# The last eighth of a down projection and the final norm, by halves of the tokens

## The chip, the cores and the metric

The kernel runs on one core of one Trainium2 chip. The metric is the device time of one execution in microseconds. The profile is one execution recorded instruction by instruction; its span reaches from the first to the last instruction.

## The reference

One layer of a hybrid block over 512 tokens of width 2048: a mixer of two recurrent head groups, a cross attention, and a squared-ReLU MLP, each added to the residual `h`, and a final norm. Only its end matters here:

```python
hn = _rmsnorm(h, norm_mlp[l])
h = h + jnp.square(jax.nn.relu(hn @ mlp_w_up[l])) @ mlp_w_down[l]     # 2048 -> 8192 -> 2048
return _rmsnorm(h, norm_final)        # h * rsqrt(mean(h*h) + eps) * gain, over the 2048 channels
```

## The kernel before

Activations lie transposed: channels on the 128 partitions, the 512 tokens along the free dimension. The residual is 16 tiles `hres[n]` (128 channels x 512 tokens, float32, `h` in the profile). All large products run in a reduced float32 format, made accurate by splitting: an operand becomes a high part `hi` (a cast, `split`, line 132, on ScalarE) and a low remainder `lo` (a subtraction, line 133, on VectorE), and a product is the sum of three matmuls: weights high by tokens high, weights high by tokens low, weights low by tokens high. All matmuls go through `mm` (line 124), so one line of the profile holds them all, and the output's name tells the stage.

`wload` (from line 150) brings one weight tile of 128 x 1024 float32 (512 KB) on the SyncE queue into one of three `wraw` buffers and splits it into `whi` and `wlo`, two buffers each. `gemm` runs the 24 matmuls of a group: 8 blocks of 128 input channels, three matmuls of 512 columns each, all into one accumulator `dn` in PSUM.

The MLP's up stage (`strassen`, output `up`) works by quarters of 256 tokens or channels and writes squared activations to DRAM (`Ud`). The down stage (`dn`) has eight eighths `e` of the 8192 hidden channels. Each eighth has 16 groups `n`, one for each residual tile; a group ends with a VectorE add of the accumulator to `hres[n]` (line 1485). While an eighth runs, `usplit` (line 1454) reads the eight token tiles of the next one from DRAM and splits them into `uh` and `ul` (128 x 512 each).

The final norm follows the last eighth: `finish` (lines 1241 to 1247) squares `hres[n]` on ScalarE and adds it to `acc` on VectorE; it starts for a tile as soon as that tile is complete. A matmul with a matrix of ones sums `acc` over the partitions (`pss`). `rsq` (lines 127 and 128) makes the reciprocal root by Ln and Exp on ScalarE, which loads a function table before each of them. Then 16 scalings on VectorE (line 1497) write to buffers `sl`, of which there are three, and SyncE stores each (line 1499, 256 KB).

The order of instructions on each engine is fixed when the kernel is built: the framework orders them by a schedule of its own, so that an operation without late inputs can come well ahead of its place in the source. An engine runs its list in order. The queue of SyncE holds loads and stores in one order; a DMA issued by ScalarE stands in ScalarE's list.

Line 1304 is the softmax exponential of the cross attention (`pr`), which uses the column tile `rcol`; line 1312 are the transposes `ptr` behind it, line 1314 their copies `phi`, and `at` is the product that uses these. The names `kp` and `sc` stand for matmuls of earlier stages.

Of the kernel before, what the change touches and what calls it, by code (L numbers as in the profile page):

```python
# [11 lines left out]
AF = mybir.ActivationFunctionType  # L12
ALU = mybir.AluOpType
# [4 lines left out]
P = 128  # L18
T = 512
M = 256  # L20
KD = 16
# [52 lines left out]
def build(tc, I, out):  # L74
    nc = tc.nc
    V, S, GP, PE = nc.vector, nc.scalar, nc.gpsimd, nc.tensor
# [19 lines left out]
    def K(name):  # L96
        o, w = CST[name]
        return cst0[:, o:o + w] if o < NC0 else cst[:, o - NC0:o - NC0 + w]

    def col(name, i=0):  # L100
        o, w = PRM[name]
        return prm[:, o + i:o + i + 1]
# [5 lines left out]
    ident, ones = K("ident"), K("ones")  # L108

    def cbias(v, nm):  # L110
        t = pc.tile([P, 1], F32, name=f"cb_{nm}")
        V.memset(t, float(v))
        return t

    b_eps6 = cbias(1e-6, "e6")
    b_gn = cbias(64e-5, "gn")
    b_one = cbias(1.0, "one")
    b_lq = cbias(-0.5 * math.log(128.0), "lq")

    def psb(nm, tag="mx", bufs=2):  # L120
        return tile_of(ps, [P, 512], F32, tag, nm, bufs)

    def mm(o, l, r, start=True, stop=True):
        PE.matmul(o, l, r, start=start, stop=stop)  # L124

    def rsq(o, x, scale, eps):
        S.activation(o, x, AF.Ln, bias=eps, scale=scale)
        S.activation(o, o, AF.Exp, scale=-0.5)

    def split(src, hi, lo, gain=None):  # L130
        if gain is None:
            S.copy(hi, src)  # L132
            V.tensor_tensor(out=lo, in0=src, in1=hi.bitcast(F32), op=ALU.subtract)  # L133
        else:
            S.activation(hi, src, AF.Copy, scale=gain)
            V.scalar_tensor_tensor(out=lo, in0=src, scalar=gain, in1=hi.bitcast(F32),
                                   op0=ALU.mult, op1=ALU.subtract)
# [4 lines left out]
    def wraw():  # L142
        wcnt[0] += 1
        return tile_of(pw, [P, 1024], F32, "wraw", f"wraw{wcnt[0]}", NWR)

    def wsplit():
        return (tile_of(pw, [P, 1024], F32R, "whi", f"whi{wcnt[0]}", NWS),
                tile_of(pw, [P, 1024], F32R, "wlo", f"wlo{wcnt[0]}", NWS))

    def wload(src):  # L150
        raw = wraw()
        nc.sync.dma_start(raw if len(src.shape) == 2 else raw.rearrange("p (a b) -> p a b", b=P), src)
        hi, lo = wsplit()
        split(raw, hi, lo)
        return hi, lo

    def gemm(pt, wsrc, nk, hi, lo):
        for h in range(nk // 8):
            wh, wl = wload(wsrc[:, h * 1024:(h + 1) * 1024] if nk > 8 else wsrc)
            for kk in range(8):  # L160
                k = h * 8 + kk
                sl = slice(kk * P, (kk + 1) * P)
                mm(pt, wh[:, sl], hi[k], start=(k == 0), stop=False)
                mm(pt, wh[:, sl], lo[k], start=False, stop=False)
                mm(pt, wl[:, sl], hi[k], start=False, stop=(k == nk - 1))
# [10 lines left out]
    def tile_of(pool, shape, dt, tag, nm, bufs):  # L176
        t = pool.tile(shape, dt, tag=tag, name=nm, bufs=bufs)
        turns[tag] = turns.get(tag, -1) + 1
        slot[t.tensor.name] = (tag, turns[tag] % bufs)
        holder[tag, turns[tag] % bufs] = t.tensor.name  # L180
        return t
# [156 lines left out]
    def act_tile(nm, dt=F32R):  # L338
        return tile_of(pa, [P, 512], dt, "act", nm, 32)
# [5 lines left out]
    rstd = pc.tile([P, T], F32, name="rstd")  # L345
# [6 lines left out]
    def tl(tag, w=512, bufs=1, shape=None):  # L352
        cnt[0] += 1
        return tile_of(pm, shape or [P, w], F32, tag, f"{tag}_{cnt[0]}", bufs)
# [53 lines left out]
    acc = tl("r")  # L408
# [763 lines left out]
    hres = [ph.tile([P, T], F32, tag=f"h{k}", name=f"h{k}", bufs=1) for k in range(16)]  # L1172
# [4 lines left out]
    def sl2(w=512):  # L1177
        cnt[0] += 1
        return ph.tile([P, 512], F32, tag="sl", name=f"sl{cnt[0]}", bufs=3)[:, 0:w]
# [18 lines left out]
    for n2 in range(8):  # L1198
        hi, lo = act_tile(f"vhi{n2}"), act_tile(f"vlo{n2}")
        for i in range(2):  # L1200
            n = 2 * n2 + i
            pt = psb(f"vp{n}", "mm", 2)
            for h in range(2):
                wh, wl = wload(I["wv"][n][:, h * 1024:(h + 1) * 1024])
                for k in range(h * 8, h * 8 + 8):
                    sl = slice(k % 8 * P, k % 8 * P + P)
# [6 lines left out]
            u, t = rstd[:, M:2 * M], sl2(M)  # L1213
# [7 lines left out]
    for g in range(4):  # L1221
        for h in range(4):
            pts = [psb(f"vo{g}_{h}_{mt}", ("mm", "mg")[h % 2]) for mt in range(2)]
            for q in range(2):
                wh, wl = wload(I["wo"][g, h][:, q * 1024:(q + 1) * 1024])
                for mt in range(2):
                    for e in range(2):
                        d = q * 2 + e
                        sl = slice(e * 512, e * 512 + 512)
# [11 lines left out]
    def finish(n, acc):  # L1241
        if n == 0:
            S.activation(acc, hres[n], AF.Square)
        else:
            sq = sl2()
            S.activation(sq, hres[n], AF.Square)
            V.tensor_tensor(out=acc, in0=acc, in1=sq, op=ALU.add)

    acc = ph.tile([P, T], F32, tag="acc", name="acc1", bufs=1)
    hh_, hl_ = [], []  # L1250
    for n in range(KD):
        xr = sl2()
        nc.sync.dma_start(xr, I["xT"][:, n, :])
        pt = psb(f"op{n}", "mm", 2)
        gemm(pt, I["w_out"][n], KD, oh, ol)
        V.tensor_tensor(out=hres[n], in0=pt, in1=xr, op=ALU.add)
        hi, lo = act_tile(f"hh{n}"), act_tile(f"hl{n}")
# [7 lines left out]
    rcol = pc.tile([P, 4], F32, name="rcol")  # L1265
# [9 lines left out]
    for g in range(2):  # L1275
        pts = [psb(f"sc{g}_{t}", ("mm", "mm", "mg", "mg")[t]) for t in range(4)]
        for n2 in range(8):
# [4 lines left out]
            wh = pw.tile([P, 1024], F32R, tag="whi", name=f"kqh{cnt[0]}", bufs=NWS)  # L1282
            wl = pw.tile([P, 1024], F32R, tag="wlo", name=f"kql{cnt[0]}", bufs=NWS)
            split(raw, wh, wl)
            for i in range(2):
                n = 2 * n2 + i
# [21 lines left out]
        for e in range(2):  # L1308
            for mt in range(2):
                pt = psb(f"ptr{g}_{e}_{mt}")  # L1310
# [9 lines left out]
    HA, HB = slice(0, M), slice(M, 2 * M)  # L1320
# [100 lines left out]
    acc = ph.tile([P, T], F32, tag="acc", name="acc2", bufs=1)  # L1421
    alloc(range(7))
    for n in range(KD):
        pt = psb(f"at{n}", "mm", 2)
# [18 lines left out]
    pu_cm = tc.tile_pool(name="pu", bufs=1, reuse_waits="tile")  # L1443
    pu = pu_cm.__enter__()
    uhl = [], []

    def usplit(f):
        if f >= 8:
            r = sl2()
        elif f % 2:  # L1450
            r = ph.tile([P, T], F32, tag="acc", name=f"ur{f}", bufs=1)
        else:
            r = pu.tile([P, T], F32, tag="ur", name=f"ur{f}", bufs=1)
        nc.sync.dma_start(r, Ud[f // 2][:, f % 2, :])
        hi, lo = act_tile(f"uh{f}"), act_tile(f"ul{f}")
        split(r, hi, lo)
        uhl[0].append(hi)
        uhl[1].append(lo)

    for p in range(32):  # L1460
        def square(i, half, c):
            t = c[:, half]
            V.scalar_tensor_tensor(out=t, in0=t, scalar=0.0, in1=rstd[:, half], op0=ALU.max, op1=ALU.mult)
            S.activation(t, t, AF.Square)
            if half is HA:
                nc.scalar.dma_start(Ud[p][:, i, :], c)

        def used(i):
            if p == 0 and i == T2:
                pt = psb("pss2")  # L1470
                mm(pt, ones, acc)
                rsq(rstd, pt, 1.0 / 2048, b_eps6)
            if p == 31 and i in (T1, T2, T3):
                for f in (range(0, 3), range(3, 6), range(6, 8))[i - T1]:
                    usplit(f)

        strassen(f"up{p}", (pu, 1024), [I["w_up"][p, i] for i in range(4)], list(range(8)), square, used)
    for e in range(8):
        uh, ul = uhl[0][e * 8:], uhl[1][e * 8:]
        for n in range(KD):  # L1480
            if e < 7 and n % 2 == 0:
                usplit(e * 8 + 8 + n // 2)
            pt = psb(f"dn{e}_{n}", "mm", 2)
            gemm(pt, I["w_dn"][e, n], 8, uh, ul)
            V.tensor_tensor(out=hres[n], in0=hres[n], in1=pt, op=ALU.add)  # L1485
    pu_cm.__exit__(None, None, None)


    acc = ph.tile([P, T], F32, tag="acc", name="acc3", bufs=1)
    for n in range(KD):  # L1490
        finish(n, acc)
    pt = psb("pss3")
    mm(pt, ones, acc)
    rsq(rstd, pt, 1.0 / 2048, b_eps6)
    for n in range(KD):
        o = sl2()
        V.scalar_tensor_tensor(out=o, in0=hres[n], scalar=col("norm_final", n), in1=rstd,
                               op0=ALU.mult, op1=ALU.mult)
        nc.sync.dma_start(out[n], o)
    es.close()  # L1500


# [96 lines left out]
```

## Time and profile before

| | us |
|---|---|
| median of 3 runs | 3080.55 (3079.55 to 3081.78) |
| the profiled execution, its own time | 3079.48 |
| its span | 3077.7 |
| mean granted TensorE clock | 0.994 |
| down stage, last matmul's end | 3053.2 |

How to read it: a row of the groups has line, engine, operation, output from inputs, shape and count, then total busy time and the mean of one in ns. A row of the chain or the timeline has the start and the length in us. A row of the windows has busy time (and count) for TensorE, its weight loads, VectorE, ScalarE and GpSimd, then the granted clock, the busy share of the DMA engines and GB/s. Matmuls overlap in the pipeline, so what a matmul costs in a stream is the distance of starts, not its length.

### The profile page before, as it was taken

What the parts mean: (1) busy time and instruction counts of PE and PEld (TensorE: products, weight loads), DVE (VectorE), ACT (ScalarE), POOL (GpSimd) and SP (SyncE); (2) the same over time, 40 slices, a digit from 0 to 9 for tenths busy, and PEclk for the clock granted to TensorE, in tenths of its full rate; (3) what the DMA queues carried; (4) which work ended last, traced back from release to release, by engine and by line L of the source; (5) the groups of instructions that cost most, each with busy time, mean ns of one, the idle gap of its engine ahead of it and who ended that gap; (6) DMA issues with size and microseconds to landing.
All of it is one profiled execution on the core that took longest, in us unless ns stands there. A gap on an engine that the chain in (4) does not pass through costs nothing.

```text
span 3077.7 us, 50561 instructions
## 1 busy us (share of the span) xinstructions
PE 3021.3 (98%) x20598; PEld 2603.3 (85%) x20598; DVE 1923.3 (62%) x2619; ACT 1331.4 (43%) x1816; POOL 575.1 (19%) x707
## 2 busy tenths in 40 slices
PE   8999999999999999999999999999999999999996
PEld 6878878888777898788878899999999888888885
DVE  6576676666667646534348899999887443344434
ACT  6445555455556555542336444444444222222222
POOL 0202302311311000000003555555552000000000
PEclk9999999999999999999999999999999999999998
DMA  5323422323425587763323343433445333333332
GB/s 174 106 82 83 107 79 79 107 79 85 134 74 154 163 272 231 257 205 123 112 92 90 124 138 124 138 130 125 138 131 167 124 115 105 126 127 123 113 96 96
DMA packets 221849, 394.73 MB, mean 128 GB/s; under 512 B 91112, under 2 KB 110828, under 8 KB 221616
## 3 DMA queue, kind: packets, MB, share of 16 engines
q1 hardware_dynamic: 207792, 366.33, 38.5%
q10 hardware_dynamic: 13824, 25.17, 2.2%
q8 instruction: 162, 2.65, 0.4%
q14 instruction: 71, 0.58, 0.1%
HBM read 343.84 MB, written 47.59 MB: 127 GB/s over the span
## 4 chain that ended last, share of the span: by engine, by line
PE 69%; DVE 2%; DMA 2%; ACT 1%; issue 0%; POOL 0%; ACTq 0%; DVEq 0%; SPq 0%; POOLq 0%
PE dn L124 23%; PE up L124 21%; PE op L124 6%; PE py L248 3%; PE vo L124 3%; PE sc L124 3%; PE kp L248 3%; PE kq L248 3%; PE at L124 2%; PE vp L124 1%; DMA mx<-mixd 1%; DVE cb L1335 0%; DMA out_dram<-sl 0%; DVE wlo L248 0%; POOL sl L1338 0%
## 5 line engine op out<-in xcount | busy, mean ns | idle before, releaser
L132 ACT CAST whi<-wraw 128x1024 fp32r<-128x1024 f32 x368 | 386.5, 1050 | 785.8 <-PE dn L124 434.1
L133 DVE TENSOR_TENSOR wlo<-wraw,whi 128x1024 fp32r<-128x1024 f32 x368 | 540.6, 1469 | 145.3 <-ACT whi L132 142.5
L124 PE MATMUL up<-cb,whi 128*128 128x256 f32 x3584 | 469.2, 284 | 4.5 <-ACT whi L132 4.5
L124 PEld LDWEIGHTS up<-cb,whi 128*128 128x128 f32 x3584 | 448.8, 193 | 5.4 <-ACT whi L132 5.3
L124 PE MATMUL dn<-uh,whi 128*128 128x512 f32 x1024 | 398.3, 389 | 0.0
L124 PE MATMUL dn<-ul,whi 128*128 128x512 f32 x1024 | 398.3, 389 | 0.0
L124 PE MATMUL dn<-uh,wlo 128*128 128x512 f32 x1024 | 398.3, 389 | 0.0
L248 PE MATMUL py<-xhi,whi 128*128 128x512 f32 x928 | 374.6, 404 | 11.7 <-ACT xhi L248 10.1
L248 PE MATMUL py<-xhi,wlo 128*128 128x512 f32 x928 | 372.5, 401 | 0.6 <-DVE wlo L248 0.5
L248 PE MATMUL py<-xlo,whi 128*128 128x512 f32 x928 | 372.2, 401 | 0.3 <-DVE xlo L248 0.3
L1485 DVE TENSOR_TENSOR h<-h,dn 128x512 f32<-128x512 f32 x128 | 88.0, 687 | 370.6 <-PE dn L124 370.6
L248 DVE TENSOR_TENSOR wlo<-wraw,whi 128x1024 fp32r<-128x1024 f32 x180 | 221.0, 1228 | 133.1 <-ACT whi L248 130.5
L248 ACT CAST whi<-wraw 128x1024 fp32r<-128x1024 f32 x180 | 188.9, 1049 | 234.3 <-PE py L248 189.1
L124 PE MATMUL up<-cb,wlo 128*128 128x256 f32 x1792 | 252.5, 284 | 1.1 <-DVE wlo L133 1.1
L124 PEld LDWEIGHTS up<-cb,wlo 128*128 128x128 f32 x1792 | 231.9, 193 | 1.4 <-DVE wlo L133 1.4
L124 PEld LDWEIGHTS dn<-uh,whi 128*128 128x128 f32 x1024 | 192.3, 188 | 39.9
L124 PEld LDWEIGHTS dn<-ul,whi 128*128 128x128 f32 x1024 | 192.3, 188 | 39.8
L124 PEld LDWEIGHTS dn<-uh,wlo 128*128 128x128 f32 x1024 | 192.3, 188 | 39.8
L248 PEld LDWEIGHTS py<-xhi,whi 128*128 128x128 f32 x928 | 175.3, 189 | 51.2 <-ACT xhi L248 10.1
L248 PEld LDWEIGHTS py<-xhi,wlo 128*128 128x128 f32 x928 | 175.1, 189 | 37.8 <-DVE wlo L248 1.7
L248 PEld LDWEIGHTS py<-xlo,whi 128*128 128x128 f32 x928 | 175.5, 189 | 34.8 <-DVE xlo L248 0.9
L133 DVE TENSOR_TENSOR wlo<-ws,whi 128x1024 fp32r<-128x1024 f32 x96 | 159.5, 1662 | 29.4 <-ACT whi L132 29.2
(688 smaller groups left out, 5296.3 us busy)
## 6 DMA issues: line engine op xcount, KB each, us to landing
wraw<-in_w_up SPq DMA_DIRECT2D x128, 512.0 KB, 4.1
wraw<-in_w_dn SPq DMA_DIRECT2D x128, 512.0 KB, 3.4
wraw<-in_w_in SPq DMA_DIRECT2D x118, 512.0 KB, 3.6
wraw<-in_wk SPq DMA_DIRECT2D x32, 512.0 KB, 3.9
wraw<-in_wqT SPq DMA_DIRECT2D x32, 512.0 KB, 4.5
wraw<-in_wv SPq DMA_DIRECT2D x32, 512.0 KB, 4.4
wraw<-in_wo SPq DMA_DIRECT2D x32, 512.0 KB, 4.2
wraw<-in_w_out SPq DMA_DIRECT2D x32, 512.0 KB, 3.9
```

The costliest lines, as they stand in the source:

```text
L124: PE.matmul(o, l, r, start=start, stop=stop)
L132: S.copy(hi, src)
L133: V.tensor_tensor(out=lo, in0=src, in1=hi.bitcast(F32), op=ALU.subtract)
L248: f(*a, **k)
L1485: V.tensor_tensor(out=hres[n], in0=hres[n], in1=pt, op=ALU.add)
```

## The change

The last eighth (`e` = 7) is taken out of the loop and run twice, for the tokens 0 to 255 (`HA`) and 256 to 511 (`HB`). Its token tiles are split by halves: `uh` holds high and low parts of the first half side by side, `ul` those of the second. For the first half (`wide`) one matmul of 512 columns multiplies the high weights with both parts, and one of 256 columns the low weights with the high part; the accumulator's two halves are both added to `hres`. For the second half three matmuls of 256 columns go into one half of the accumulator. The weights of the eighth are loaded and split once for each half. Behind each half follows its norm: squares, sum (the last square goes to a second matmul instead of to `acc`), `rsq`, scalings in place in `hres`, and stores of 128 x 256, alternately from SyncE's and ScalarE's queue. Behind the first half's `rsq` stands one Ln on one column, written to `rcol`.

```diff
-        split(r, hi, lo)
+        if f < 56:
+            split(r, hi, lo)
+        else:
+            for t, half in ((hi, HA), (lo, HB)):
+                split(r[:, half], t[:, HA], t[:, HB])
...
-    for e in range(8):
+    for e in range(7):
...
+    def last(n, half, wide):
+
+        pt = psb(f"dn7_{n}", "mm", 2)
+        wh, wl = wload(I["w_dn"][7, n])
+        u = uhl[half is HB][56:]
+        h = hres[n][:, half]
+        for k in range(8):
+            sl = slice(k * P, k * P + P)
+            if wide:
+                mm(pt, wh[:, sl], u[k], start=k == 0, stop=False)
+            else:
+                mm(pt[:, HA], wh[:, sl], u[k][:, HA], start=k == 0, stop=False)
+                mm(pt[:, HA], wh[:, sl], u[k][:, HB], start=False, stop=False)
+            mm(pt[:, HA], wl[:, sl], u[k][:, HA], start=False, stop=k == 7)
+        V.tensor_tensor(out=h, in0=h, in1=pt[:, HA], op=ALU.add)
+        if wide:
+            V.tensor_tensor(out=h, in0=h, in1=pt[:, HB], op=ALU.add)
+
+    acc = ph.tile([P, T], F32, tag="acc", name="acc3", bufs=1)
+    for half in (HA, HB):
+        for n in range(KD):
+            last(n, half, half is HA)
+            sq = acc[:, half] if n == 0 else sl2(M)
+            S.activation(sq, hres[n][:, half], AF.Square)
+            if 0 < n < KD - 1:
+                V.tensor_tensor(out=acc[:, half], in0=acc[:, half], in1=sq, op=ALU.add)
+        pt = psb("pss3")[:, HA]
+        mm(pt, ones, acc[:, half], start=True, stop=False)
+        mm(pt, ones, sq, start=False, stop=True)
+        rsq(rstd[:, half], pt, 1.0 / 2048, b_eps6)
+        if half is HA:
+            S.activation(rcol[:, 0:1], b_one, AF.Ln)
+        for n in range(KD):
+            h = hres[n][:, half]
+            V.scalar_tensor_tensor(out=h, in0=h, scalar=col("norm_final", n), in1=rstd[:, half],
+                                   op0=ALU.mult, op1=ALU.mult)
+            (nc.sync if n % 2 else nc.scalar).dma_start(out[n][:, half], h)
...
-    acc = ph.tile([P, T], F32, tag="acc", name="acc3", bufs=1)
-    for n in range(KD):
-        finish(n, acc)
-    pt = psb("pss3")
-    mm(pt, ones, acc)
-    rsq(rstd, pt, 1.0 / 2048, b_eps6)
-    for n in range(KD):
-        o = sl2()
-        V.scalar_tensor_tensor(out=o, in0=hres[n], scalar=col("norm_final", n), in1=rstd,
-                               op0=ALU.mult, op1=ALU.mult)
-        nc.sync.dma_start(out[n], o)
```

In the prediction, A0 to A15 and B0 to B15 are the 16 groups of the first and the second half.

More of the change, by code (lines that the diff above doesn't have):

```diff
@@ L1477, in build @@
         strassen(f"up{p}", (pu, 1024), [I["w_up"][p, i] for i in range(4)], list(range(8)), square, used)
-    for e in range(8):
+    for e in range(7):
         uh, ul = uhl[0][e * 8:], uhl[1][e * 8:]
         for n in range(KD):
-            if e < 7 and n % 2 == 0:
+            if n % 2 == 0:
                 usplit(e * 8 + 8 + n // 2)
```

## The prediction

> **What bounds the kernel now.** The page first: one line for the span, one for TensorE.
>
> ```profile
> span 3077.7 us, 50561 instructions
> PE 3021.3 (98%) x20598; PEld 2603.3 (85%) x20598; DVE 1923.3 (62%) x2619; ACT 1331.4 (43%) x1816; POOL 575.1 (19%) x707
> ```
>
> TensorE is the bound, and a busy row of 98% leaves about 56 us without it. Where do they lie near the change? The chain that ended last gives the whole down stage in one piece, and, asked again for the end, the tail behind it.
>
> ```profile
> 2356.86 696.36 PE dn L124 x3072
> ```
>
> ```profile
> 3053.24 0.70 DVE h L1485
> 3054.02 0.64 ACT sl L1246
> 3055.43 1.14 PE pss L124 x2
> 3056.59 0.69 ACT rstd L127
> 3057.30 1.28 ACT L128
> 3059.26 0.76 DVE sl L1497
> 3060.04 2.06 DMA out_dram<-sl
> 3062.19 0.76 DVE sl L1497
> ...
> 3073.85 0.75 DVE sl L1497
> ```
>
> 3072 matmuls of 512 columns in 696.36 us are 0.2267 us each, with nothing between them: the last eighth (384 of them) is 87.05 us of unbroken TensorE. Behind it, from 3053.22 to the end of the span, 24.5 us have no matmul work but one sum over partitions. 6.0 us of these go from the last matmul to the first scaling (add, square, sum, Ln, table load, Exp), 15.3 us to the scalings, which run three at a time and then wait for a store to free one of the three `sl` buffers (scaling at 3059.26, next trio only at 3062.19), and 3.1 us from the last scaling's end (3074.60) to 3077.7.
>
> **The change part by part.** Times by their rows first: the groups by form for the end of the kernel; then one line's instructions each for the 256-column forms (minimum, median and maximum in ns), a trio of scalings in the timeline, and two windows.
>
> ```profile
> L133 DVE TENSOR_TENSOR wlo<-wraw,whi 128x1024 fp32r<-128x1024 f32 x18 | 22.1, 1225 | 3.7 <-ACT whi L132 3.7
> L132 ACT CAST whi<-wraw 128x1024 fp32r<-128x1024 f32 x18 | 19.0, 1053 | 72.1 <-issue 50.2 <-PE dn L124 21.9
> L1485 DVE TENSOR_TENSOR h<-h,dn 128x512 f32<-128x512 f32 x20 | 13.7, 687 | 58.7 <-PE dn L124 58.7
> L1497 DVE SCALAR_TENSOR_TENSOR sl<-h,prm,rstd 128x512 f32<-128x512 f32 x16 | 11.3, 750 | 8.0 <-DMA out_dram<-sl 4.1 <-ACT rstd L128 3.9
> L127 ACT ACT_TABLE_LOAD x1 | 1.3, 1283 | 0.0
> ```
>
> ```profile
> L1463 DVE SCALAR_TENSOR_TENSOR sl<-sl,rstd x128: 406/414/2402, 1726.0 to 2359.1; 128x256 f32<-128x256 f32 x128
> L1384 DVE TENSOR_TENSOR sl<-sl,up x224: 403/408/422, 1720.4 to 2357.0; 128x256 f32<-128x256 f32 x112
> L1464 ACT ACTIVATE sl<-sl x128: 407/417/421, 1728.4 to 2359.5; 128x256 f32<-128x256 f32 x128
> L1466 ACTq DMA_DIRECT2D ud<-sl x64: 326/326/327, 1730.7 to 2360.0; - x64
> 3059.26 2.08 DVE L1497 SCALAR_TENSOR_TENSOR sl<-h,prm,rstd 128x512 f32<-128x512 f32 x3 [3.88 <-ACT rstd L128]
> 3061.00:3062.00 1.00, 0.00 (x0) 0.00 (x0) 0.34 (x1) 0.00 (x0) 0.00 (x0) 0.50 1.00 377
> 1703.00:1704.00 1.00, 0.66 (x6) 0.47 (x5) 0.93 (x2) 0.44 (x2) 1.00 (x2) 1.00 1.01 406
> ```
>
> In the last two rows, windows of 1 us, the last columns are the busy share of the DMA engines and what they moved: 377 GB/s from the old stores (rows of 2 KB, one queue), 406 from weight loads (rows of 4 KB), each with the engines full.
>
> *TensorE's own work.* Half A is 8 pairs per group, one matmul of 512 columns (weights high, tokens high and low side by side) and one of 256. Half B is 24 matmuls of 256. The same columns stream as before, but in 640 instructions instead of 384, and all 16 weight tiles come twice. This trace has both patterns: the `kp` stage alternates 512 and 256, and the up stage runs 256 alone.
>
> ```profile
> 939.68 0.39 PE L248 MATMUL kp<-mhl,whi 128*128 128x512 f32 x1
> ...
> 941.80 0.39 PE L248 MATMUL kp<-mhl,whi 128*128 128x512 f32 x1
> 1800.00:1900.00 100.00, 100.00 (x836) 100.00 (x835) 91.58 (x91) 44.86 (x60) 52.71 (x21) 1.00 0.40 132
> ```
>
> Six pairs from 939.68 to 941.80 are 0.353 us a pair; 836 matmuls in 100 us are 0.1196 us. Half A: 16 x 8 x 0.353 = 45.2. Half B: 384 x 0.1196 = 45.9. Together 91.1 against 87.05: **+4.1** (3.6 to 4.6).
>
> *Do the other engines keep up?* A group of half A lasts 2.83 us. VectorE does in it two adds and one sum (3 x 0.41) and one weight remainder (1.23): 2.46, so it keeps up with 0.37 to spare; ScalarE (1.05 + 0.42) does easily. Half B has one add less. The reloaded weights are 512 KB per 2.83 us, 185 GB/s, under half of what the windows show; with three `wraw` buffers a load is issued over two groups ahead of its cast. The eight token tiles of the last eighth split in halves add some 0.1 us an operation under groups of 5.4 us that TensorE fills: nothing. So these cost nothing as long as that 0.37 holds; each 0.1 us beyond it would cost 16 x 0.1 = 1.6.
>
> *The seam between the halves.* Here the order in which the changed kernel is built decides: on VectorE the 16 scalings of half A stand ahead of the adds of groups B0 and B1, and these ahead of the weight remainder of B2. On TensorE only the two sums over partitions (together the columns of the one that took 1.14: 1.1 us), B0 and B1 (2 x 2.87) and the first pairs of B2 and B3 (0.5) stand ahead of that remainder: 7.3 us of work. From the last matmul of half A to its last Exp: 0.2 to the first add, two adds 0.75, square 0.5, Ln's table 1.28, Ln 0.48 (0.69 less the 0.22 that half the columns save: a square took 0.64 at 512, 0.42 at 256), Exp's table 1.28, Exp 0.42, with some 0.1 of hand-overs 5.0 us. A scaling with a column operand took 0.75 at 512 columns and three of them 2.08, a pitch of 0.66; half the columns save as much as on an add (an add takes 0.69 at 512, 0.41 at 256: 0.28), so 0.39 each and 16 x 0.39 = 6.2. Then two adds 0.7 and the remainder 1.23: 13.2 us. TensorE stands 13.2 - 7.3 = **+5.9** (4.9 if a scaling takes 0.33, as far below `L1463`'s 0.41 as the pitch of the trio lies below 0.75; 7.3 if 0.48), and the sums themselves are **+1.1** of its time. The eight stores that ScalarE issues here (0.33 each) hold its casts of B2 and B3 back, which are still ready before VectorE is; the eight on SP stand ahead of the weight load of B5, which is needed 7 us later. Covered, both; without VectorE's delay the casts would end last, at about 10 us.
>
> *The clock after that gap.* The timeline's and the windows' rows (the third figure from their end is the granted clock) for a gap of 5.96 us of this trace, then for a second one:
>
> ```profile
> 948.16 0.58 PE L248 MATMUL kp<-mhl,wlo 128*128 128x256 f32 x1 [5.96 <-DVE wlo L248]
> 947.00:948.00 1.00, 0.00 (x0) 0.00 (x0) 1.00 (x1) 0.23 (x1) 0.00 (x0) 0.58 0.62 179
> 953.00:954.00 1.00, 1.00 (x5) 0.90 (x4) 0.00 (x0) 0.00 (x0) 0.76 (x4) 0.50 0.43 176
> 954.00:955.00 1.00, 1.00 (x7) 0.87 (x7) 0.00 (x0) 0.37 (x2) 0.81 (x3) 1.00 0.03 12
> ```
>
> ```profile
> 1709.00:1710.00 1.00, 0.42 (x2) 0.42 (x3) 1.00 (x1) 0.53 (x1) 1.00 (x1) 0.50 0.00 0
> 1714.51 2.08 PE L124 MATMUL up<-cb,wlo 128*128 128x256 f32 x8 [1.15 <-DVE wlo L133]
> 1718.00:1719.00 1.00, 1.00 (x8) 1.00 (x7) 0.91 (x1) 0.00 (x0) 1.00 (x1) 0.71 0.00 0
> ```
>
> After 5.96 us idle the granted clock was 0.50 and stayed so for 5.8 us of work (948.16 to 954.0); after the second gap, with a further stop of 1.15 us, for 9 us (1709.6 to 1718.6). Half clock loses half of that. The seam's gap is as long as the first, so I take somewhat under its 2.9: **+2.4** (1.5 to 4.5). The Trainium skill, "TensorE: Matmul & The Clock Gate", "Part 1: The HAM clock gate", says that the gate judges by a free-running window of 3.4 us and opens after about 3.4 us of sustained work; an estimate by that page is 1.7 instead of 2.4, a total 0.7 lower. Both gaps here took longer than that budget, so by the trace I stay at 2.4.
>
> *The tail.* After half B the same chain has 256 columns: one add 0.41, square, Ln's table (now exposed: square's end to the sum's end is only 0.6), Ln, table, Exp: 4.5 us after the last matmul's end the first scaling starts, where it was 6.0. Scaling in place takes the wait for buffers away: 15 x 0.39 + 0.48 = 6.3 where it was 15.3. The end stays 3.1. 13.9 against 24.5: **-10.6**. The second queue adds issue slots only: one queue already filled the engines in the window at 3061. What counts is the row length. 377 and 406 GB/s are, on one of 16 engines, 87 ns for a row of 2 KB and 161 ns for one of 4 KB; a straight line gives 50 ns for the new rows of 1 KB. 16 stores of 128 rows on 16 engines: 6.4 us, as long as the scalings. Nothing to add (bounds -0.3 and +4.8, below).
>
> *The preload of Ln.* The one-column Ln written behind half A's norm, which should load the table for the end, reads nothing that comes late, and the build puts it far ahead: into the softmax of the second head pair, between two of its exponentials. There it costs two table loads and a small Ln.
>
> ```profile
> 1610.53 0.55 ACT L1304 ACTIVATE pr<-sc,nb,rcol 128x256 f32<-128x256 f32 x1
> 1612.41 0.56 ACT L1304 ACTIVATE pr<-sc,nb,rcol 128x256 f32<-128x256 f32 x1 [1.24 <-DVE nb L1301]
> 1617.77 0.73 PE L124 MATMUL at<-phi,whi 128*128 128x512 f32 x2 [0.62 <-ACT phi L1314]
> L128 ACT ACTIVATE rcol<-rcol x1: 205/205/205, 1523.3 to 1523.3; 128x4 f32<-128x4 f32 x1
> ```
>
> From 1611.1: 1.28 + 0.2 + 1.28 ends at 1613.9, where the next exponential began at 1612.41; the idle 1.24 before that is cover. From there ScalarE and VectorE hand on to each other up to the matmul at 1617.77, which already waits for ScalarE: **+1.5** (1.0 to 2.0), and no cover follows, since TensorE is busy from there.
>
> *Sum.* 4.1 + 1.1 + 5.9 + 2.4 - 10.6 + 1.5 = +4.4 us. On the profiled execution's 3079.48 (span 3077.7 and 1.8 around it) this is 3083.9; the median of the runs is 1.1 above that execution, so 3085.0.
>
> **The rivals.** *Short rows, slower.* If a row of 1 KB costs an engine the 87 ns of a 2 KB row, the last 16 stores take 11.1 us instead of 6.3 and end 4.8 later: +9.2, 3089.8. It decides from 49 ns a row on. For it: the two measured sizes leave the fixed part of a row open, and no row shows 1 KB alone. Against: 161 and 87 ns lie nearly in proportion to size. *Clock and scalings long, slower.* If the clock stays low for 9 us as at 1709.6, 4.5 instead of 2.4 is lost, and a scaling of 0.42 adds 0.5 at the seam and 0.5 at the end: +7.5, 3088.0. For it: the second gap; against: nothing stops TensorE after B2, so a full busy stretch follows at once. It passes 0.2% from a total loss 1.8 above mine on. *No stall.* If the seam were covered after all, its 5.9 and 2.4 would go: -3.9, 3076.6. Against it: 16 scalings cannot start before the Exp, and B2's remainder stands behind them. Even without the preload's 1.5 this is 3075.1, so over 0.2% faster needs a further gain that no row shows. *The preload hidden*, that is the change not doing that harm: 3083.5.
>
> **How the numbers follow.** 0.2% is 6.2 us, about what a measurement of this kernel can tell from no change: 3074.4 to 3086.7. Forecast with the hidden preload 0.54; short rows 0.18; long clock and scalings 0.22; no stall 0.06, half of it over the bound. So within 0.57, slower 0.40, faster 0.03. The forecast's own range is 3082.5 to 3086.7; to hold 8 in 10 it reaches over both slower rivals, 3081.5 to 3090.0.
>
> **What would show it.** Right: a single TensorE gap of about 5 us, 7 us after half A's last matmul, ended by B2's `wlo`, and granted clock 0.5 behind it; half A at 2.83 and half B at 2.87 us a group; the last matmul near 3068; first to last scaling about 6 us with no wait for a store; two extra table loads between exponentials near 1611 and the `at` matmuls 1.5 us later. Wrong: groups of half A above 2.9 us (VectorE the bound), stores landing more than 2.5 us after the last scaling (short rows), or no gap at the seam.

## The result and the profile after

| | us |
|---|---|
| before, median of 21 runs | 3080.55 (3078.88 to 3082.69) |
| after, median of 21 runs | 3085.53 (3082.88 to 3088.11) |
| ratio after to before | 1.0015, 95% interval 1.0009 to 1.0020 |
| profiled execution after, its own time and span | 3085.53, 3083.7 |

The change makes the kernel 5.0 us slower, within the 0.2% that the prediction named. Two lines of the page of the changed kernel:

```profile
span 3083.7 us, 51305 instructions
PE 3027.7 (98%) x20860; PEld 2616.1 (85%) x20860; DVE 1959.9 (64%) x2704; ACT 1357.0 (44%) x1863; POOL 575.0 (19%) x707
```

As before, a share of 98% says little; the chain of waits shows where the time went (start, length, what):

```profile
2360.26 654.41 PE dn L124 x2943
...
3019.69 2.54 DVE h L1526 x7
...
3026.12 0.66 DVE h L1506 x2
3026.78 1.15 DVE wlo L133
...
3027.98 41.81 PE dn L124 x332
...
3074.29 2.07 DVE h L1526 x5
...
3076.75 3.96 DVE h L1526 x10
```

What was one piece of 696.36 us is now two, with ScalarE's and VectorE's work between them. The down stage runs from 2360.26 to 3069.79: 709.5 us, **+13.2**. From there to the end of the span it is 13.9 us where it was 24.5: **-10.6**. The order around the `at` matmuls of the attention costs **+1.6** (below). These three make +4.2, which lies in the interval of the ratio (+2.8 to +6.2 us). The two profiled executions differ by 6.0 us; 2.6 of that has arisen before the first `ptr` transposes of that place (1609.24 before, 1611.83 after), where all operations and their order are the same, and 0.8 is made up again between the `at` matmul and the down stage (the executions lie 4.2 apart at the one, 3.4 at the other).

The seam, in the timeline of TensorE and then of VectorE (start, length, operation; in brackets the idle time before it and what ended it):

```profile
3014.62 0.70 PE L124 MATMUL pss<-acc,cst 128*128 128x256 f32 x2
3016.22 0.67 PE L124 MATMUL pss<-sl,cst 128*128 128x256 f32 x2
3026.60 1.19 PE L124 MATMUL dn<-ul,whi 128*128 128x256 f32 x4 [5.05 <-DVE h L1506]
3027.98 0.58 PE L124 MATMUL dn<-ul,wlo 128*128 128x256 f32 x1 [0.18 <-DVE wlo L133]
```

```profile
3019.69 6.43 DVE L1526 SCALAR_TENSOR_TENSOR h<-h,prm,rstd 128x256 f32<-128x256 f32 x16 [2.65 <-ACT rstd L128]
3026.03 0.75 DVE L1506 TENSOR_TENSOR h<-h,dn 128x256 f32<-128x256 f32 x2
3026.69 1.23 DVE L133 TENSOR_TENSOR wlo<-wraw,whi 128x1024 fp32r<-128x1024 f32 x1
```

Half A's last matmul ends where `pss` begins, at 3014.62. TensorE has work until 3021.55 and then stands for 5.05 us: 16 scalings (6.43 us) stand on VectorE ahead of the two adds that free the accumulators and of B2's `wlo`. The long gap ends with the first of these adds, since B2's first pair needs an accumulator; `wlo` ends a second, short one. The windows of 1 us (granted clock, DMA share and GB/s are the last three columns) show what follows, and what the stores do meanwhile:

```profile
3023.00:3024.00 1.00, 0.00 (x0) 0.00 (x0) 1.00 (x3) 0.24 (x1) 0.00 (x0) 1.00 1.00 334
3025.00:3026.00 1.00, 0.00 (x0) 0.00 (x0) 1.00 (x3) 0.00 (x0) 0.00 (x0) 0.51 0.97 326
3031.00:3032.00 1.00, 1.00 (x7) 1.00 (x7) 0.00 (x0) 0.00 (x0) 0.00 (x0) 0.58 0.82 238
3032.00:3033.00 1.00, 1.00 (x10) 1.00 (x9) 0.39 (x1) 0.50 (x1) 0.00 (x0) 1.00 0.49 201
```

The clock falls to half in the gap and comes back only just before 3032: 5.25 us after TensorE's restart, with 7 matmuls in the microsecond of which a part is already at full clock (0.58 over the slice), and 10 in the next. The DMA engines, full with rows of 1 KB, move 334 GB/s, that is 49 ns a row.

The tail, in the timeline of all engines:

```profile
3069.81 0.42 DVE L1506 TENSOR_TENSOR h<-h,dn 128x256 f32<-128x256 f32 x1 [1.49 <-PE dn L124]
3070.76 1.28 ACT L127 ACT_TABLE_LOAD   x1
3074.29 6.42 DVE L1526 SCALAR_TENSOR_TENSOR h<-h,prm,rstd 128x256 f32<-128x256 f32 x16 [4.06 <-ACT rstd L128]
3074.80 5.88 ACTq L1528 DMA_DIRECT2D out_dram<-h  x8
3075.20 5.87 SPq L1528 DMA_DIRECT2D out_dram<-h  x8
```

The 16 scalings run without a wait, and Ln's table load lies on the chain. Where the line meant to hide that load went is seen in ScalarE's timeline, 1.45 ms earlier:

```profile
1613.12 0.56 ACT L1304 ACTIVATE pr<-sc,nb,rcol 128x256 f32<-128x256 f32 x1
...
1613.79 1.28 ACT L1523 ACT_TABLE_LOAD   x1
1615.08 0.20 ACT L1523 ACTIVATE rcol<-cb_one 128x1 f32<-128x1 f32 x1
1615.30 1.28 ACT L1304 ACT_TABLE_LOAD   x1
1616.60 0.56 ACT L1304 ACTIVATE pr<-sc,nb,rcol 128x256 f32<-128x256 f32 x1
```

Between two exponentials of the softmax stand two loads. TensorE's timeline there:

```profile
1611.83 0.41 PE L1312 MATMUL ptr<-cst,pr 128*128 128x128 f32 x2 [0.29 <-DVE nb L1301]
...
1621.95 0.74 PE L124 MATMUL at<-phi,whi 128*128 128x512 f32 x2 [0.79 <-ACT phi L1314]
```

The stretch from the `ptr` transposes (1611.83) to the `at` matmul that waits for `phi` (1621.95) is 10.12 us; before, it was 1609.24 to 1617.77, 8.53.

### The profile page after: what moved, and what is told of

Its sections match the earlier page's. It is cut to its first block, busy times and chain, and to the rows that moved or that the text cites. A ratio compares the mean times of both kernels' runs of the same rounds, so it can differ in the third digit from the quotient of the medians.

```text
span 3083.7 us, 51305 instructions
## 1 busy us (share of the span) xinstructions
PE 3027.7 (98%) x20860; PEld 2616.1 (85%) x20860; DVE 1959.9 (64%) x2704; ACT 1357.0 (44%) x1863; POOL 575.0 (19%) x707
## 4 chain that ended last, share of the span: by engine, by line
PE 67%; DVE 3%; DMA 2%; ACT 2%; issue 1%; POOL 0%; DVEq 0%; ACTq 0%; SPq 0%; POOLq 0%
PE dn L124 23%; PE up L124 20%; PE op L124 6%; PE py L248 3%; PE sc L124 3%; PE vo L124 3%; PE kp L248 3%; PE kq L248 3%; PE at L124 2%; DMA mx<-mixd 2%; PE vp L124 1%; DVE wlo L133 1%; DVE cb L1335 0%; DVE h L1526 0%; DVE ol L133 0%
## 5 line engine op out<-in xcount | busy, mean ns | idle before, releaser
L132 ACT CAST whi<-wraw 128x1024 fp32r<-128x1024 f32 x384 | 403.4, 1050 | 780.9 <-PE dn L124 459.2
L133 DVE TENSOR_TENSOR wlo<-wraw,whi 128x1024 fp32r<-128x1024 f32 x384 | 563.9, 1468 | 148.6 <-ACT whi L132 143.9
L124 PE MATMUL dn<-ul,whi 128*128 128x512 f32 (+1 forms) x1152 | 397.1, 368 | 5.0 <-DVE h L1506 5.0
L124 PE MATMUL dn<-uh,wlo 128*128 128x512 f32 (+1 forms) x1024 | 384.5, 375 | 0.0
L248 DVE TENSOR_TENSOR wlo<-wraw,whi 128x1024 fp32r<-128x1024 f32 x180 | 221.5, 1230 | 134.8 <-ACT whi L248 131.5
L248 ACT CAST whi<-wraw 128x1024 fp32r<-128x1024 f32 x180 | 188.9, 1050 | 236.4 <-PE py L248 188.8
L1489 DVE TENSOR_TENSOR h<-h,dn 128x512 f32<-128x512 f32 x112 | 77.0, 687 | 328.3 <-PE dn L124 328.3
L124 PEld LDWEIGHTS dn<-ul,whi 128*128 128x128 f32 x1152 | 209.9, 190 | 40.2 <-issue 5.2
```

What stands on the lines that cost most here:

```text
L248: f(*a, **k)
```

## The experiments

Each was timed beside the kernel before on the same chip, 11 runs against 15 to 33. The ratio's interval is about 2.7 us to either side, so that effects of 1 to 2 us are read from the stretches of the trace, and the ratio says whether their sum holds. "Down" is the down stage, "tail" from its end to the end of the span, "at" the stretch of the attention; "sum" adds their differences to the kernel before. The last two columns are the ratio, with its interval, and the difference that it makes on 3080 us.

| kernel | down | tail | at | sum | ratio | measured |
|---|---|---|---|---|---|---|
| before | 696.4 | 24.5 | 8.5 | | | |
| after | 709.5 | 13.9 | 10.1 | +4.2 | 1.0015 (1.0009 to 1.0020) | +4.6 |
| `nopre` | 710.0 | 14.2 | 8.5 | +3.3 | 1.0012 (1.0003 to 1.0021) | +3.7 |
| `lateln` | 709.9 | 13.5 | 8.5 | +2.5 | 1.0010 (1.0001 to 1.0019) | +3.1 |
| `seam` | 703.6 | 13.9 | 10.1 | -1.8 | 1.0000 (0.9991 to 1.0009) | 0.0 |
| `both` | 703.6 | 13.6 | 8.5 | -3.7 | 0.9989 (0.9981 to 0.9998) | -3.4 |
| `warm` | 708.1 | 13.9 | 10.1 | +2.7 | 1.0009 (1.0001 to 1.0018) | +2.8 |
| `oneq` | 709.7 | 15.1 | 10.1 | +5.5 | 1.0020 (1.0011 to 1.0029) | +6.2 |
| `inplace` | 696.4 | 20.4 | 8.5 | -4.1 | 0.9983 (0.9975 to 0.9992) | -5.2 |
| `inplace2q` | 696.4 | 20.2 | 8.5 | -4.3 | 0.9983 (0.9974 to 0.9992) | -5.2 |
| `best` | 696.4 | 18.7 | 8.5 | -5.8 | 0.9982 (0.9973 to 0.9991) | -5.5 |

**The preload of Ln.** `nopre` takes the line out:

```diff
-        if half is HA:
-            S.activation(rcol[:, 0:1], b_one, AF.Ln)
```

> The changed kernel without its early Ln on one column. My theory (the build has put that Ln with two table loads between two exponentials of the attention, where ScalarE is waited for): both table loads near 1613 go, the stretch from the exponential behind them to the product that waits for ScalarE is 1.5 to 1.6 us shorter, and the time is 1.6 us less than the changed kernel's 3085.5, about 3084.0 (3.4 above before). The end is the same: 4.5 us from the last matmul to the first scaling, since the preload never reached it. Rival (it was hidden there): 3085.5, no difference in that stretch. Second rival (it did serve the end): 4.5 us become longer, and the time is not less.

TensorE's timeline at the same place:

```profile
1611.43 0.41 PE L1312 MATMUL ptr<-cst,pr 128*128 128x128 f32 x2 [0.29 <-DVE nb L1301]
...
1619.96 0.73 PE L124 MATMUL at<-phi,whi 128*128 128x512 f32 x2 [0.62 <-ACT phi L1314]
```

The stretch in the attention is 8.53 us again, and the chain of the tail is as long as with the line (4.5 us from the last matmul's end to the first scaling): the line cost 1.6 us and gave nothing. The down stage's 0.5 more lies behind the seam, where the clock came back later after `wlo` (332 matmuls in 42.27 us, which took 41.81 in the changed kernel); the tail's 0.3 lies behind the last scaling (3.3 us to the end of the span instead of 3.0). So the stretches together give 0.9 us less than the changed kernel, where 1.6 was expected. `lateln` gives the Ln an input that is ready late, a column of the ninth square of half B:

```diff
+            if half is HB and n == 8:
+                S.activation(rcol[:, 0:1], sq[:, 0:1], AF.Ln)
...
-        if half is HA:
-            S.activation(rcol[:, 0:1], b_one, AF.Ln)
```

> The changed kernel with that Ln made to read the square of group B8, so that it cannot be built ahead of it. My theory: the 1.5 to 1.6 us near 1613 go, and at the end Ln no longer waits for a table: 4.5 us from the last matmul to the first scaling become 3.9. 2.2 us less than the changed kernel in all: 3083.3. ScalarE has 1.4 us to spare in a group of 2.87, so the load inside half B costs at most 0.1. Rival (the sum over partitions, not the table, ends last in front of Ln): only 1.6 less, 3083.9, and 4.5 us stay.

Its tail, in the timeline:

```profile
3068.51 0.42 DVE L1506 TENSOR_TENSOR h<-h,dn 128x256 f32<-128x256 f32 x1 [1.49 <-PE dn L124]
...
3070.23 0.47 ACT L127 ACTIVATE rstd<-pss,cb_e 128x256 f32<-128x256 f32 x1 [0.79 <-PE pss L124]
...
3072.47 2.86 DVE L1526 SCALAR_TENSOR_TENSOR h<-h,prm,rstd 128x256 f32<-128x256 f32 x7 [3.54 <-ACT rstd L128]
```

From the add to the first scaling 3.96 us instead of 4.48: no table load stands ahead of Ln, which now waits for `pss`. A load is 1.28 us, but only 0.52 came out, as the rest lay beside the sum over partitions. The squares after that Ln needed no other table. All in all the stretches give 1.7 us less than the changed kernel, not 2.2: the down stage's 0.4 more is a single wait for a `wlo` near 2370, in code that the edit leaves as it was.

**The seam.** `seam` leaves half A's norm where it is and writes its scalings, each with its store, behind the groups B2 to B15, one behind each and three behind the last two:

```diff
...
+            if half is HB and n >= 2:
+                scale(n - 2, HA)
+                if n >= KD - 2:
+                    scale(n, HA)
...
```

> The changed kernel with half A's scalings written between the groups of half B instead of in one row ahead of them; as built, three stand ahead of the add of B0 and five ahead of the weight remainder of B2. My theory (VectorE's row of 16 scalings makes the 5 us gap, and the gap halves the clock for 5 us behind it): the remainder of B2 is ready about 8.5 us after half A's last matmul instead of 13.2, TensorE stands 1.5 us there and some 0.5 at B3, the granted clock stays 1.0, and the time is 6 us less than the changed kernel: 3079.5 (3078.5 to 3080.5). Rival (the clock costs nothing by itself): only 4 less, 3081.5. Rival (another wait takes its place, the weight loads behind the stores on SyncE): under 2 less, and gaps in half B that end on a cast waiting for a load.

TensorE's timeline and a window behind the seam:

```profile
3021.76 0.28 PE L124 MATMUL dn<-ul,wlo 128*128 128x256 f32 x1
3022.26 0.51 PE L124 MATMUL dn<-ul,whi 128*128 128x256 f32 x2 [0.23 <-ACT whi L132]
3023.76 0.39 PE L124 MATMUL dn<-ul,wlo 128*128 128x256 f32 x1 [0.99 <-DVE wlo L133]
3023.99 0.40 PE L124 MATMUL dn<-ul,whi 128*128 128x256 f32 x2
```

```profile
3024.00:3025.00 1.00, 1.00 (x10) 1.00 (x10) 1.00 (x4) 0.50 (x2) 0.00 (x0) 1.00 0.25 61
```

Of the gap, 0.23 and 0.99 us are left, and the clock stays at 1.00. The down stage is 5.9 us shorter than in the changed kernel, as expected, and the time equals the kernel before. This shows that the place of the scalings made the gap: they were moved, with their stores, and nothing else. The stores were not what TensorE waited for in the changed kernel: the last weight cast that they hold back ended at 3024.80, VectorE's two adds only at 3026.78. `both` joins it with `lateln`:

> The scalings between the groups of half B and the late Ln together. If the two act in different places, their gains add: 6 + 2.2 below the changed kernel, 3077.3 (3.2 below before, 0.1%). Rival (one of them only moves the wait that the other shows): no less than the better of the two alone.

The down stage of the one and the attention and tail of the other come out together, and it is a little faster than the kernel before (0.9989, 0.9981 to 0.9998). Whether the halves earn any of that is another question, taken up with `inplace`.

**The clock by itself.** `warm` fills the gap instead of removing it, with 48 matmuls that do no work of the reference:

```diff
+            if half is HB and n == 1:
+                dm = psb("warm", "mg")
+                for z in range(48):
+                    mm(dm[:, HA], uhl[0][56][:, 0:P], uhl[1][56][:, HA], start=z == 0, stop=z == 47)
```

> The changed kernel with 48 additional matmuls of 256 columns (48 x 0.12 = 5.8 us) on TensorE behind group B1, from loaded token tiles into a PSUM buffer that nothing reads; they do no work of the reference, and fill the gap at the seam. Theory (the gap costs twice, once idle and once by the clock): the granted clock stays at 1.00 through B2 and B3, these groups take 2.88 us each, and the down stage is 2.4 us (2 to 2.9) shorter than in the changed kernel, whose gap is otherwise still there; the time about 2.5 us above the kernel before. Rival (the clock after the gap costs nothing by itself, since B2 to B4 wait for VectorE's weight remainders anyway): down stage as in the changed kernel, within 0.5 us.

TensorE's timeline, a window in the filled gap, and the piece of the chain behind it:

```profile
3027.74 0.40 PE L124 MATMUL dn<-ul,whi 128*128 128x256 f32 x2
3028.56 0.38 PE L124 MATMUL dn<-ul,wlo 128*128 128x256 f32 x1 [0.41 <-DVE wlo L133]
```

```profile
3024.00:3025.00 1.00, 1.00 (x11) 1.00 (x10) 1.00 (x3) 0.65 (x1) 0.00 (x0) 1.00 0.98 329
```

```profile
3028.56 40.35 PE dn L124 x334
```

The clock stayed at 1.00, and the down stage is 1.4 us shorter than in the changed kernel, not 2.4: a miss in size, though not the rival's 0.5. From B2's `wlo` on, 332 matmuls took 41.81 us in the changed kernel; here 334 took 40.35, so 332 would take 40.11: 1.7 us lost to the clock after `wlo`. (As built, the changed kernel has two matmuls more ahead of `wlo`, 0.24 us, so that the down stages differ by 1.4.) The other part of the half-clock time, 3026.60 to 3027.98, lay under the wait for `wlo`, which comes 13.3 us after half A's end in both kernels.

**The queues.** `oneq` stores everything from SyncE:

```diff
-            (nc.sync if n % 2 else nc.scalar).dma_start(out[n][:, half], h)
+            nc.sync.dma_start(out[n][:, half], h)
```

> The changed kernel with all 32 stores from SyncE's queue. Theory: SyncE issues a store in about 0.35 us, so 16 take 5.6 us, under the 6.4 of the scalings: tail 13.9 us and time as the changed kernel, 5 us above the kernel before. At the seam 16 instead of 8 stores stand ahead of the weight load of B5, which is still in time. Rival (one queue is bound by its issues at 1 KB rows, or B5's load comes late): the tail or the down stage over 0.5 us longer than in the changed kernel.

My theory fell here. A window of the tail, and the row of the stores' line from 3060 on (durations of an issue in ns, first and last start):

```profile
3076.00:3077.00 1.00, 0.00 (x0) 0.00 (x0) 1.00 (x3) 0.00 (x0) 0.00 (x0) 0.50 0.79 265
```

```profile
L1528 SPq DMA_DIRECT2D out_dram<-h x16: 343/399/450, 3072.8 to 3080.1; - x16
```

16 issues span 7.3 us, 0.49 from one to the next, not 0.35; the DMA engines are busy for 0.79 and move 265 GB/s, and the tail is 1.2 us longer. With two queues (above) 8 issues of 332 to 343 ns each kept pace with the scalings, and the window at 3079 of the changed kernel has 1.00 and 337 GB/s. At the seam the one queue did no harm: down 709.7 against 709.5.

`inplace` and `inplace2q` ask the same of 256 KB stores, in the kernel before:

```diff
-        o = sl2()
-        V.scalar_tensor_tensor(out=o, in0=hres[n], scalar=col("norm_final", n), in1=rstd,
+        o = hres[n]
+        V.scalar_tensor_tensor(out=o, in0=o, scalar=col("norm_final", n), in1=rstd,
```

> The kernel before with one edit: the final scalings write to hres in place instead of to the three sl buffers; everything else, the single store queue too, stays. Theory (waiting for buffers made the old tail long): the 16 scalings of 512 columns take 16 x 0.665 = 10.7 us instead of 15.3. A scaling makes 256 KB in 0.665 us, 394 GB/s, a little over the 377 GB/s of the full engines, so the stores set the pace at 0.695 us each, 11.1 us for 16. The end comes 4 us earlier (3 to 5) than in the kernel before. Rival (the stores themselves, not the buffers, take the time): no change, within 0.5 us.

> As the in-place edit alone, with the stores alternately from SyncE's and ScalarE's queue. Theory: one queue fills the engines already, so a second one adds nothing: the tail within 0.3 us of the in-place edit alone. Rival (a queue of its own limits): the tail at least 1 us shorter than with one queue.

The scalings of `inplace`, its stores, and a window:

```profile
3061.32 10.69 DVE L1497 SCALAR_TENSOR_TENSOR h<-h,prm,rstd 128x512 f32<-128x512 f32 x16 [4.12 <-ACT rstd L128]
```

```profile
3062.10 10.27 SPq L1499 DMA_DIRECT2D out_dram<-h  x16
```

```profile
3064.00:3065.00 1.00, 0.00 (x0) 0.00 (x0) 1.00 (x3) 0.00 (x0) 0.00 (x0) 0.50 1.00 375
```

16 scalings in a row, 10.69 us instead of 15.3; the DMA engines full from one queue; the tail 4.1 us shorter. With two queues it is 20.2, the same within the 0.3 expected. So the second queue is worth 1.2 us at 128 KB a store and nothing at 256 KB. More than that: one small part of the change, alone, makes the kernel faster (0.9983, 0.9975 to 0.9992), adds nothing to the down stage, and gains by the stretches as much as `both` does with the halves (4.1 against 3.7).

**A shorter end without halves.** `best` adds to `inplace` a chain in which only the last group's add, square and sum go by halves, the last square goes straight to the sum, and Ln's table is loaded at the ninth square:

```diff
...
+        if n == 8:
+            S.activation(rcol[:, 0:1], acc[:, 0:1], AF.Ln)
+    for half in (HA, HB):
+        sq = sl2(M)
+        S.activation(sq, hres[KD - 1][:, half], AF.Square)
+        pt = psb("pss3")[:, HA]
+        mm(pt, ones, acc[:, half], start=True, stop=False)
+        mm(pt, ones, sq, start=False, stop=True)
+        S.activation(rstd[:, half], pt, AF.Ln, bias=b_eps6, scale=1.0 / 2048)
+    S.activation(rstd, rstd, AF.Exp, scale=-0.5)
...
```

> The kernel before with the in-place scalings on one queue, and the end of its norm shortened without splitting the eighth: only the last group's add, its square and its sum run by halves of the tokens, the last square goes to a second sum over partitions instead of to acc, and Ln's table is loaded at the ninth square by an Ln on one column of acc. Theory (the chain's length is what its instructions take in a row): from the last matmul's end to the first scaling 4.4 us (0.43 first add, 0.4 and 0.42 squares, 0.65 sum, 0.47 Ln, 1.28 table, 0.65 Exp, some 0.1 of hand-overs) instead of 6.3; the down stage unchanged at 696.4 us; tail 18.6 us instead of the 20.45 of the in-place edit alone; time 5.9 us below the kernel before. Rival (the chain is bound elsewhere, or the early Ln delays squares that the last groups wait for): no gain over the in-place edit, 4 us below the kernel before or less.

Its chain of waits:

```profile
2357.59 696.36 PE dn L124 x3072
...
3053.97 0.43 DVE h L1486
...
3055.69 0.91 ACT rstd L1501 x2
...
3056.61 1.28 ACT L1502
...
3058.57 3.40 DVE h L1505 x5
```

4.6 us from the last matmul's end to the first scaling, where `inplace` took 6.3; the tail is 18.7. By time it can't be told from `inplace` (their intervals are nearly the same); the 1.7 us are the trace's, and 0.24 of them are a slower sum over partitions in `inplace` (1.38 us, where the kernel before took 1.14). It beats the kernel before and the changed one.

## Why the prediction was right

The forecast was 3085.0 us with +4.4 against the profiled execution; measured 3085.53, by the three stretches +4.2. The total agrees better than the terms do: the clock was taken 0.6 us too high, and the streaming, the gap and the preload 0.1 to 0.2 too low each, and that is partly luck. The terms, one by one:

- *TensorE's own work*, +4.1: right. From start to start, half A took 45.22 us (2969.40 to 3014.62); in half B the adds of the groups come every 2.88 us, 46.1 in all: +4.3 with 87.05 taken off. The two sums over partitions, +1.1, were 1.0 (6.66 us from 3014.62 to the start of B1's last matmul at 3021.28, less 47 matmuls at 0.12). VectorE kept up with half A, at 2.83 us a group.
- *The seam's gap*, +5.9: right in size. The forecast is the time until `wlo` lets TensorE go on, less the work ahead of it; measured, that is 13.36 us (3014.62 to 3027.98) less 7.26 (the sums and 52 matmuls at 0.12), or 6.1. The place and the length of the list on VectorE (13.3 us, forecast 13.2) were as named, and `seam` shows the cause. One step was wrong: it took the first pairs of B2 and B3 for work that fills the wait, with a single gap ended by `wlo`. They had to wait for an accumulator, so the long gap (5.05 us) was ended by the add, and only 0.18 by `wlo`. This cost nothing more, as the pairs ran while `wlo` was still being made.
- *The clock*, +2.4: the half-clock time behind the restart was 5.25 us, near the 5.8 on which I based it, but its price by experiment is 1.4 to 1.7 us, and what is left in half B for it is 1.8 (41.63 us from `wlo` to the next sum over partitions at 3069.61, less 332 matmuls at 0.12). The step that failed is the one that halved the whole half-clock time: a part of it passed while TensorE was waiting for `wlo` anyway. The Trainium skill, "TensorE: Matmul & The Clock Gate", "Part 1: The HAM clock gate", gives a budget of about 3.4 us at the low clock. The trace doesn't agree on the time (5.25 us); that the estimate of 1.7 by that page came nearer in price is chance, since it halves a shorter time, where in the trace a part of a longer one cost nothing. Nor is 5.25 fixed: behind the same gap (5.0 us) the clock came back 5.2 us after the restart in `lateln`, 5.7 in `oneq` and 6.3 in `nopre`. Together gap and clock were 8.3 in the forecast and 7.9 in the trace (half B's 54.99 us, 3014.62 to 3069.61, less 46.1 and 1.0).
- *The tail*, -10.6: right to 0.1 us, chain 4.5, scalings 6.4, the rest 3.0. Rows of 1 KB cost 49 ns, so the rival with 87 ns fell. But one sentence in it was wrong: that the second queue adds nothing. I took it from stores of 256 KB; for 128 KB one queue issues too slowly, and without the second the tail would have been 1.2 us longer.
- *The preload*, +1.5: measured 1.6, and `nopre` shows it. The Trainium skill, "ScalarE: Activation LUTs", section "What ACT_TABLE_LOAD costs", gives a switch of tables 1283 ns and a drain of some 1380 ns more. The first figure is the trace's; the second isn't seen here: the load starts at 1613.79 and the Ln behind it at 1615.08.
- *The rivals.* A long low clock and slow scalings: neither came, the scaling's pitch was 0.40 and the clock was low for 5.25 us, not 9. No stall: it takes another order on VectorE, as `seam` has it. The hidden preload: `nopre` and `lateln` are that case, forecast 2.9 above the kernel before and found at +3.3 and +2.5 by the stretches.

What the prediction had not asked is which part of the change earns its 10.6 us. The experiments split it: scaling in place, 4.1, needs no halves; a shorter chain, 1.7, doesn't either. Only the rest, some 4.8 us (18.7 against 13.9, most of it in the row of scalings, 10.7 against 6.4), is bought by halving, for 5.3 us of additional streaming and sums and whatever the seam costs.

With `seam`, half B still takes 2.0 us more than its matmuls and sums. The idle times shown in its two waits are only 1.2, but by the starts the waits explain 1.75: from 3021.76 to 3023.99 there are four matmuls in 2.23 us, where the stream has 0.12 each. The remaining 0.2 are two hesitations of about 0.1 us, near 3026.75 and 3035.4. What stays open is whether halving can earn anything over `best`: the stretches say no for the orders tried (-3.7 for `both`, -5.8 for `best`), but the intervals of their ratios overlap.

## What to carry to other kernels

Split a change into its edits before costing it: here the cheapest of them, writing in place, held the safe gain, and the structural one around it cost more than it gave. When work is interleaved at a seam, look at the list of the engine that is not the bound: what is written behind a long run of cheap operations waits for all of them, unless they are dealt out between the groups. And a preload needs an input that comes late, or a scheduler can put it where it does harm.

## What the runs showed of the hardware

- One queue issues 128 KB stores every 0.49 us (265 GB/s with the DMA engines at 0.79), two queues fill them (320 to 337 GB/s in the tail); at 256 KB a store one queue is enough (375 GB/s).
- A row of 1 KB costs a DMA engine 49 ns, near the 50 ns that a straight line through the 87 ns and 161 ns of rows of 2 and 4 KB gives.
- After a gap of 5.05 us the granted clock stayed at half for 5.25 us after TensorE's restart (5.2 to 6.3 us behind the same gap in other runs), at a price of 1.4 to 1.7 us; matmuls without use in the gap kept it at 1.00.
- A table load of ScalarE took 1.28 us; taking the one ahead of the last Ln out of the chain gave back 0.52 us, what it did not share with the sum over partitions.
